# Expert weights in runs of 32 KB a partition, in pools opened on the mixer's bytes, in a hybrid encoder layer

## The chip, the cores and the metric

The kernel runs on one core of one Trainium2 chip. The metric is the device time of one execution in microseconds (us); the median of the runs counts. The engines are TensorE (PE in the rows; PEld is its weight load), VectorE (DVE), ScalarE (ACT), GpSimd (POOL) and SyncE (SP), whose queue issues nearly all transfers. Each transfer is spread over the core's 16 DMA engines.

## What is computed

One post-norm layer of an encoder on 512 tokens of 1024 columns, all in float32. A mixer (windowed attention and a short convolution, both gated) is followed by a LayerNorm and a routed mixture of 16 experts, in which each expert takes its 64 best tokens; a LayerNorm ends the layer.

```python
x = layer_norm(x, ln0_g, ln0_b)
h = hybrid_mixer(x, ...)                       # projections, attention, convolution, gates, output
x = layer_norm(DEEPNORM_ALPHA * x + h, ...)
aff = softmax(x @ w_router); top_val, top_idx = top_k(aff over tokens, 64)
xe = x[top_idx]                                # 16 experts x 64 tokens
h = silu(xe @ w_gate) * (xe @ w_up)            # 1024 -> 2048
ye = (h @ w_down) * top_val                    # 2048 -> 1024
x = layer_norm(DEEPNORM_ALPHA * x + scatter_add(ye, top_idx), ...)
```

The experts' weights are 16 x 3 x 8 MB, that is 402.7 MB, and each is read once.

## The kernel before, in words

**The mixer** streams its weights in chunks of 1 MB through two buffers called raw, splits each into a high and a low half (ws), and multiplies. Its tiles of 8 KB a partition have names: Z0 to Z3, Y0 to Y3, O0 to O3, M0 to M3, two raw, two ws; beside them stand X0 and X1 (the tokens), W0 to W2 (scratch), and E.

**The experts** are worked through in 8 pairs, one expert in each half of TensorE's columns. A pair has 48 weight units of 1 MB (8 KB a partition, 128 partitions). Units 0 to 31 are gate and up weights, in turn, in four blocks cb of eight; units 32 to 47 are the down weights, in four blocks cq of four. I number them on through the pairs, so that pair 1 begins with unit 48. For each unit `fetch` or `fetch_down` (lines 596 to 602) takes the next place of a list, `ring` (line 580), has SP load the unit into it (line 593), and TensorE multiplies it (line 933 for gate and up, 973 for down). The places of the ring are the mixer's tiles themselves, 20 of them, with E, W0 and W2; W0 and W2 are used once. Unit 0 goes into E, 1 to 4 into Z0 to Z3, 5 and 6 into ws, 7 and 9 into raw, 8 into W2, 10 into W0, 11 to 22 into Y, M and O and M3; unit 23 goes into E again, unit 24 into Z0, and so on round the ring. Two places leave it behind the first down block (line 984) and become `acc`, the sum of the experts' outputs. A load waits on SP until the last reader of its place is done, and since every load is pinned in program order on SP's one queue, the loads behind it wait too.

Between the units a list `pend` gives TensorE small pieces of other work: the gather of the next pair's tokens (line 869, two pieces ahead of the down units, the rest at the next pair's start), the transposes of the hidden rows (956), and the scatter of each finished down block (990) whose result VectorE adds to `acc` (995).

**The end.** In the last pair the last unit is loaded in three pieces, and the sums of the last 256 columns don't pass through `acc`: in cq 2 four multiplications with the identity (line 980) put `acc`'s last 256 columns into four PSUM tiles `ends`, one for each 128 tokens, and line 1007 adds the last scatter to them. The last LayerNorm reads them (1010 on), and SP and ACT store the rows.

Of the kernel before, what the change touches and what calls it, by code (L numbers as in the profile page):

```python
# [18 lines left out]
P = 128  # L19
D = 1024  # L20
# [17 lines left out]

@with_exitstack
def encoder_layer(ctx: ExitStack, tc: tile.TileContext, x, ln0r, ln0c, w_in, conv_w, sink, w_ao, w_co, w_out,  # L40
                  ln1r, ln1c, w_router, w_gate, w_up, w_down, ln2r, out):
    nc = tc.nc
    const = ctx.enter_context(tc.tile_pool(name="const", bufs=1))
    xpool = ctx.enter_context(tc.tile_pool(name="xpool", bufs=1))
# [23 lines left out]
    def pst(name):  # L68
        return psp.tile([P, 512], F32, tag="ps", name=name)
# [32 lines left out]
    iota = const.tile([P, CAP], F32, name="iota")  # L102
    nc.gpsimd.iota(iota, pattern=[[1, CAP]], base=1, channel_multiplier=0, allow_small_or_imprecise_dtypes=True)

    spools = {}
    for n in ("Z0", "M", "O", "Y", "raw", "ws", "Z"):
        spools[n] = ctx.enter_context(tc.tile_pool(name=f"p{n}", bufs=2 if n in ("raw", "ws") else 1))
    rawp, wsp = spools["raw"], spools["ws"]

    def slot(tag, shape, name, dt=F32):  # L110
        return shaped((xpool if tag[0] == "X" else spools.get(tag) or spools[tag[0]]).tile([P, 2048], dt, tag=tag, name=name), shape)

    class Pair:

# [462 lines left out]
    for t in range(NT):  # L577
        hooks[(f"gc{t // 2 + 1}_{t % 2}", 0)] = [entry(t)]

    ring = ["E"] + [f"Z{i}" for i in range(4)] + ["ws", "ws", "raw", "W2", "raw", "W0"] + "Y0 Y1 Y2 Y3 M0 M1 M2 O0 O1 O2 O3 M3".split()  # L580

    def ring_slot(shape, name):
        tag = ring.pop(0)
        pool = {"ws": wsp, "raw": rawp, "E": extra}.get(tag) or (wk if tag[0] == "W" else spools.get(tag) or spools[tag[0]])
        return tag, shaped(pool.tile([P, 2048], F32, tag=tag, name=name), shape)

    ahead = {}

    def load(src, key):
        tag, c = ring_slot(list(src.shape[1:]), "w_" + "_".join(map(str, key)))  # L590
        if tag[0] != "W":
            ring.append(tag)
        pin(nc.sync.dma_start(c, src))
        return c

    def fetch(p, cb, kq, i):
        key = (p, cb, kq, i)
        return ahead.pop(key) if key in ahead else load((w_gate, w_up)[i][p, cb, kq], key)

    def fetch_down(p, cq, fq):  # L600
        for f, n in ((0, 2), (2, 1), (3, 1)) if (p, cq, fq) == (NPAIR - 1, 3, 3) else ((0, 4),):
            yield load(w_down[p, cq, fq][:, :, f:f + n, :], (p, cq, fq, f, "d")), 4 * fq + f

    def early():
        ahead[0, 0, 0, 0] = fetch(0, 0, 0, 0)

    hooks[("gc3_0", 2)] = [early]

# [242 lines left out]
    nc.vector.tensor_tensor(tied, mask[:, NT - 1:, 1, :], counts[:, :, 1, :], OP.mult)  # L851
    nc.vector.tensor_tensor(place, place, tied, OP.add)

    def gather(p):
        e = slice(2 * p, 2 * p + 2)
        px = wkt(1 + 2 * p, [2048], f"px_{p}")
        xe = px[:, 0:1024].rearrange("p (k c) -> p k c", k=KT)
        ohT = px[:, 1024:1536]
        oh1 = px[:, 1536:2048].rearrange("p (t a c) -> p t a c", t=NT, a=2)
        for t in range(NT):  # L860
            nc.vector.tensor_tensor(oh1[:, t], iota[:, None, :].to_broadcast([P, 2, CAP]),  # L861
                                    place[:, t, e, None].to_broadcast([P, 2, CAP]), OP.is_equal)

        def take(k, n):
            def go():
                ps = pst(f"g_{p}_{k}")
                for i in range(n):
                    for t in range(NT):
                        pin(nc.tensor.matmul(ps[:, i * P:(i + 1) * P], xt[t][:, (k + i) * P:(k + i + 1) * P],  # L869
                                             oh1[:, t].rearrange("p a c -> p (a c)"), start=(t == 0), stop=(t == NT - 1)))  # L870
                dst = xe[:, k:k + n, :].rearrange("p k c -> p (k c)")
                if p:
                    nc.scalar.copy(dst, ps[:, :n * P])
                elif k % 2:
                    nc.vector.tensor_scalar(dst, ps[:, :P], cols[:, 2, k:k + 1], cols[:, 3, k:k + 1], op0=OP.mult, op1=OP.add)
                else:
                    nc.scalar.activation(dst, ps[:, :P], AF.Identity, bias=cols[:, 3, k:k + 1], scale=cols[:, 2, k:k + 1])
            return go

        def rest():  # L880
            nc.vector.tensor_tensor(oh1, oh1, aff[:, :, e, None].to_broadcast([P, NT, 2, CAP]), OP.mult)
            ps = pst(f"oht_{p}")
            for t in range(NT):
                pin(nc.tensor.transpose(ps[:, t * P:(t + 1) * P], oh1[:, t].rearrange("p a c -> p (a c)"), ident))
            nc.scalar.copy(ohT, ps)
        return xe, ohT, [take(k, 2 if p else 1) for k in range(0, KT, 2 if p else 1)] + [rest]
# [32 lines left out]
        nxt[2].pop(0)()  # L919
    for p in range(NPAIR):  # L920
        last = p == NPAIR - 1
        xe, ohT, takes = nxt
        pend[:0] = takes
        for cb in range(NCB):
            pss = [mmt(f"p{nm}_{p}_{cb}") for nm in "gu"]
            for kq in range(4):
                for i in range(2):
                    wt = fetch(p, cb, kq, i)
                    for k in range(2):
                        kk = 2 * kq + k  # L930
                        for a in range(2):
                            hs = slice(64 * a, 64 * a + 64)
                            pin(nc.tensor.matmul(pss[i][hs, :], xe[:, kk, hs], wt[:, a, k, :], start=(kk == 0), stop=(kk == KT - 1)))  # L933
                    for _ in range(2 * i if p == cb == 0 else 1 - i):
                        if pend:
                            pend.pop(0)()
            if p == 0 and cb == 1:
                ln1 = wkt(0, [2, D], "ln1")
                nc.scalar.dma_start(ln1[0:1], ln1r[None])
                pend.extend(spread(ln1))  # L940
                pend.append(affine)
            if last and cb == 1:
                ln2 = wkt(2, [2, D], "ln2")
                nc.scalar.dma_start(ln2[0:1], ln2r[None])
                pend.extend(spread(ln2))
            hb = tmpt([512], f"h_{p}_{cb}")
            nc.scalar.activation(hb, pss[0], AF.Silu)  # L947
            nc.vector.tensor_tensor(hb, hb, pss[1], OP.mult)  # L948

            def turn(cb=cb, hb=hb, p=p):  # L950
                if cb == 0:
                    hTs[p] = wkt(2 + 2 * p, [FF // P, P], f"hT_{p}")
                hT = hTs[p]
                ps = pst(f"ht_{p}_{cb}")
                for i in range(4):
                    pin(nc.tensor.transpose(ps[:, i * P:(i + 1) * P], hb[:, i * P:(i + 1) * P], ident))
                nc.scalar.copy(hT[:, 4 * cb:4 * cb + 4, :].rearrange("p k c -> p (k c)"), ps)

            pend.append(turn)
        if not last:  # L960
            nxt = gather(p + 1)
            for _ in range(2):
                nxt[2].pop(0)()
            flush()
        for cq in range(4):
            pd = mmt(f"d_{p}_{cq}")
            for fq in range(4):
                for wt, f0 in fetch_down(p, cq, fq):
                    for ft in range(wt.shape[2]):
                        f = f0 + ft  # L970
                        for a in range(2):
                            hs = slice(64 * a, 64 * a + 64)
                            pin(nc.tensor.matmul(pd[hs, :256], hTs[p][:, f, hs], wt[:, a, ft, :], start=(f == 0), stop=(f == 15)))  # L973
                for _ in range(2):
                    if pend:
                        pend.pop(0)()
                if last and cq == 2 and fq >= 2:
                    for t in range(2 * fq - 4, 2 * fq - 2):
                        ends.append(pst(f"end{t}")[:, :256])
                        pin(nc.tensor.matmul(ends[t], ident, acc[t // 2][:, t % 2, 768:1024], start=True, stop=False))  # L980
            ye = tmpt([256], f"ye_{p}_{cq}")
            nc.scalar.copy(ye, pd[:, :256])  # L982
            if p == 0 and cq == 0:
                acc = [ring_slot([2, D], f"acc{i}")[1] for i in range(2)]

            def scatter(t, p=p, cq=cq, ye=ye, ohT=ohT):
                def go():
                    cs = slice(cq * 256, (cq + 1) * 256)
                    ps = (mmt if p == NPAIR - 1 and cq == 2 else pst)(f"sc_{p}_{cq}_{t}")
                    pin(nc.tensor.matmul(ps[:, :256], ohT[:, t * P:(t + 1) * P], ye, start=True, stop=True))  # L990
                    a = acc[t // 2][:, t % 2, cs]
                    if p == 0:
# [11 lines left out]


    for t in range(NT):
        pin(nc.tensor.matmul(ends[t], ohT[:, t * P:(t + 1) * P], ye, start=False, stop=True))
    for t in range(NT + 1):
        if t < NT:
            pin(nc.vector.bn_stats(st2[:, t, 3, :], ends[t]))  # L1010
# [84 lines left out]
```

## Time and profile before

| | |
|---|---|
| median of 3 runs | 1471.23 us (1469.98 to 1474.84) |
| the profiled execution | 1471.5 us, of it a span of 1469.8 us from the first to the last instruction |
| TensorE busy | 1386.3 us, 94% of the span |
| DMA | 451.13 MB, mean 307 GB/s |
| chain that ended last | PE 49%, DMA 47% |
| loads of the experts' weights | 383 of 1 MB or less in the rows by kind, median 19.9 us from issue to landing |

A busy TensorE in this profile is not TensorE at its peak: the ends of multiplications are modelled. What bounds a stage is read from the rate of the DMA engines in it and from what the engines' waits ended with.

### The profile page before, as it was taken

What the parts mean: (1) busy time and instruction counts of PE and PEld (TensorE: products, weight loads), DVE (VectorE), ACT (ScalarE), POOL (GpSimd) and SP (SyncE); (2) the same over time, 40 slices, a digit from 0 to 9 for tenths busy, and PEclk for the clock granted to TensorE, in tenths of its full rate; (3) what the DMA queues carried; (4) which work ended last, traced back from release to release, by engine and by line L of the source; (5) the groups of instructions that cost most, each with busy time, mean ns of one, the idle gap of its engine ahead of it and who ended that gap; (6) DMA issues with size and microseconds to landing.
All of it is one profiled execution on the core that took longest, in us unless ns stands there. A gap on an engine that the chain in (4) does not pass through costs nothing.

```text
span 1469.8 us, 18064 instructions
## 1 busy us (share of the span) xinstructions
PE 1386.3 (94%) x7559; PEld 810.6 (55%) x7559; DVE 396.8 (27%) x892; ACT 291.8 (20%) x580; POOL 61.8 (4%) x46
## 2 busy tenths in 40 slices
PE   8999999999999999999999998998998899899985
PEld 6878778788888843643644632542452353264243
DVE  7566656633335530110110110110010011010015
ACT  5654454422233211000001000000000000000100
POOL 3000000320000004000000000000000000000001
PEclk9999999999999999999999999999999999999998
DMA  4221222322237879999999999999999999999993
GB/s 146 97 76 58 87 86 87 115 99 102 86 143 295 327 297 379 419 419 420 419 419 420 418 419 420 419 419 420 419 420 419 419 419 420 419 419 419 420 420 153
DMA packets 67205, 451.13 MB, mean 307 GB/s; under 512 B 7730, under 2 KB 10418, under 8 KB 13234
## 3 DMA queue, kind: packets, MB, share of 16 engines
q1 hardware_dynamic: 65824, 446.28, 75.1%
q10 hardware_dynamic: 1300, 3.70, 0.7%
q8 instruction: 59, 0.97, 0.3%
q14 instruction: 22, 0.18, 0.0%
HBM read 447.86 MB, written 2.10 MB: 306 GB/s over the span
## 4 chain that ended last, share of the span: by engine, by line
PE 49%; DMA 47%; DVE 3%; ACT 1%; issue 0%; SPq 0%; DVEq 0%
DMA w<-in_w_gate 26%; DMA w_d<-in_w_down 14%; DMA w<-in_w_up 7%; PE d L973 5%; PE pu L933 4%; PE pg L933 4%; PE p_x L181 3%; PE p_b L181 3%; PE p_c L181 3%; PE p_q L181 3%; PE p_co L181 3%; PE p_ao L181 3%; PE p_gc L181 3%; PE p_ga L181 3%; PE g L869 2%; PE o L521 1%
## 5 line engine op out<-in xcount | busy, mean ns | idle before, releaser
L933 PE MATMUL pg<-w,px 128*64 128x512 f32 x1024 | 245.0, 598 | 33.1 <-DMA w<-in_w_gate 32.8
L933 PE MATMUL pu<-w,px 128*64 128x512 f32 x1024 | 246.9, 603 | 15.3 <-DMA w<-in_w_up 15.3
L973 PE MATMUL d<-w_d,hT 128*64 128x256 f32 x2048 | 237.7, 383 | 7.4 <-DMA w_d<-in_w_down 7.3
L973 PEld LDWEIGHTS d<-w_d,hT 128*64 128x64 f32 x2048 | 142.7, 137 | 94.4 <-issue 19.0
L933 PEld LDWEIGHTS pg<-w,px 128*64 128x64 f32 x1024 | 69.1, 136 | 192.4 <-issue 101.3
L933 PEld LDWEIGHTS pu<-w,px 128*64 128x64 f32 x1024 | 64.7, 136 | 145.6 <-issue 96.7
L995 DVE TENSOR_TENSOR acc<-acc,sc 128x256 f32<-128x256 f32 x108 | 45.5, 421 | 330.5 <-PE sc L990 330.1
L948 DVE TENSOR_TENSOR h<-h,pu 128x512 f32<-128x512 f32 x32 | 22.0, 688 | 344.7 <-PE pu L933 344.7
L947 ACT ACTIVATE h<-pg 128x512 f32<-128x512 f32 x32 | 19.1, 597 | 331.5 <-PE pg L933 331.5
L990 PE MATMUL sc<-ye,px 128*128 128x256 f32 x248 | 73.8, 411 | 0.0
L869 PEld LDWEIGHTS g<-px,xn 128*128 128x128 f32 x512 | 59.0, 192 | 20.5 <-issue 17.9
L982 ACT COPY ye<-d 128x256 f32<-128x256 f32 x32 | 11.9, 372 | 276.7 <-PE d L973 276.7
L990 PEld LDWEIGHTS sc<-ye,px 128*128 128x128 f32 x248 | 40.8, 188 | 43.7 <-issue 41.2
L869 PE MATMUL g<-px,xn 128*128 128x128 f32 x512 | 63.8, 280 | 0.2 <-DVE px L861 0.2
L181 PE MATMUL p_x<-yh,ws_x 128*128 128x512 f32 x128 | 43.9, 398 | 0.0
L181 PE MATMUL p_b<-yh,ws_b 128*128 128x512 f32 x128 | 43.9, 398 | 0.0
L181 PE MATMUL p_c<-yh,ws_c 128*128 128x512 f32 x128 | 43.7, 397 | 0.0
L181 PE MATMUL p_q<-yh,ws_q 128*128 128x512 f32 x128 | 42.1, 395 | 0.0
L493 ACT ACTIVATE pr<-pr,neg 128x256 f32<-128x256 f32 (+1 forms) x64 | 35.2, 553 | 28.7 <-DVE neg L489 28.7
L181 PE MATMUL p_ga<-yh,ws_ga 128*128 128x512 f32 x128 | 40.6, 391 | 0.0
L181 PE MATMUL p_gc<-yh,ws_gc 128*128 128x512 f32 x128 | 40.1, 389 | 0.0
L181 PE MATMUL p_ao<-oh,ws_ao 128*128 128x512 f32 x128 | 40.1, 389 | 0.0
(264 smaller groups left out, 1619.8 us busy)
## 6 DMA issues: line engine op xcount, KB each, us to landing
w<-in_w_gate SPq DMA_DIRECT2D x128, 1024.0 KB, 19.9
w<-in_w_up SPq DMA_DIRECT2D x128, 1024.0 KB, 19.9
w_d<-in_w_down SPq DMA_DIRECT2D x127, 1024.0 KB, 19.9
raw_q<-in_w_in SPq DMA_DIRECT2D x4, 1024.0 KB, 4.8
raw_c<-in_w_in SPq DMA_DIRECT2D x4, 1024.0 KB, 4.8
raw_x<-in_w_in SPq DMA_DIRECT2D x4, 1024.0 KB, 4.9
raw_b<-in_w_in SPq DMA_DIRECT2D x4, 1024.0 KB, 4.9
raw_ga<-in_w_in SPq DMA_DIRECT2D x4, 1024.0 KB, 4.7
```

The lines of the kernel that those rows point to most:

```text
L181: put(nc.tensor.matmul(ps, ws[:, a, k, :], (opnd.lo if b else opnd.hi)(k), start=(k + a + b == 0), stop=ends))
L493: nc.scalar.activation(p, p, AF.Exp, bias=self.neg[:, i:i + 1], accum_out=self.su[:, i:i + 1])
L521: nc.tensor.matmul(pa[half * 64:half * 64 + 64, :256], vt[g][:, self.b0 + j, :], self.pT[:, j, :, half, :], start=(j == 0), stop=(j == sel ...
L869: pin(nc.tensor.matmul(ps[:, i * P:(i + 1) * P], xt[t][:, (k + i) * P:(k + i + 1) * P], oh1[:, t].rearrange("p a c -> p (a c)"), start=(t ...
L933: pin(nc.tensor.matmul(pss[i][hs, :], xe[:, kk, hs], wt[:, a, k, :], start=(kk == 0), stop=(kk == KT - 1)))
L947: nc.scalar.activation(hb, pss[0], AF.Silu)
L948: nc.vector.tensor_tensor(hb, hb, pss[1], OP.mult)
L973: pin(nc.tensor.matmul(pd[hs, :256], hTs[p][:, f, hs], wt[:, a, ft, :], start=(f == 0), stop=(f == 15)))
L982: nc.scalar.copy(ye, pd[:, :256])
L990: pin(nc.tensor.matmul(ps[:, :256], ohT[:, t * P:(t + 1) * P], ye, start=True, stop=True))
L995: nc.vector.tensor_tensor(a, a, ps[:, :256], OP.add)
```

## The change

The three weight arrays become one, `w_moe`, laid out by pair and by group of four units, so that a group is one contiguous run of 32 KB in each partition (8 KB before).

- **Places.** The mixer's tiles get a pool each (ws and raw one each of two buffers), in the order Z0 to Z3, ws, raw, Y, M0 to M2, O, M3. Behind the routing all of them are closed, and on their bytes 20 places of 8 KB are opened: R0 and R1 in a pool that stays open, R2 to R19 in 18 pools of one. Every new tile waits for the tiles whose bytes it takes, not for whole pools ("reuse_waits").
- **Pair 0** goes on in units of 8 KB: 1 to 7 in R0 to R6, 8 in W2, 9 in R7, 10 in W0, 11 to 22 in R8 to R19, 23 in E, 24 to 41 in R2 to R19, 42 in E, 43 to 47 in R2 to R6. R0 and R1 take no second unit; they become `acc`.
- **From pair 1 on** R2 to R19 are closed and one pool of four buffers of 32 KB is opened there. A group of four units is one tile; its load of 4 MB is issued when its first unit is wanted. In the last pair, groups 4 to 11 are loaded by unit (8 KB a partition) into such a tile, and the last unit in three pieces as before.
- **The last sums.** The four multiplications with the identity become two of 512 columns, put into `pend` behind block cb 2 of the last pair; two blocks of 128 tokens share a PSUM tile. The scatters of the last pair's cq 2 take their PSUM from the other pool.

```diff
-    for n in ("Z0", "M", "O", "Y", "raw", "ws", "Z"):
-        spools[n] = ctx.enter_context(tc.tile_pool(name=f"p{n}", bufs=2 if n in ("raw", "ws") else 1))
+    mixer = ExitStack()
+    for n in "Z0 Z1 Z2 Z3 ws raw Y0 Y1 Y2 Y3 M0 M1 M2 O0 O1 O2 O3 M3".split():
+        spools[n] = mixer.enter_context(tc.tile_pool(name=f"p{n}", bufs=2 if n in ("raw", "ws") else 1))
...
+    UNITS = 48
+    units, groups = {}, {}
+
+    def load_unit(p, m, pool, tag):
+        t = pool.tile([P, 2048], F32, tag=tag, name=f"w_{p}_{m}")
+        pin(nc.sync.dma_start(t, w_moe[p, m // 4][:, m % 4]))
+        return t
+
+    def fetch(p, m):
+
+        if p == 0:
+            if m not in units:
+                units[m] = load_unit(0, m, *places.pop(0))
+            return units.pop(m)
+        g, j = m // 4, m % 4
+        if j == 0:
+            t = big[0].tile([P, 4, 2048], F32, tag="G", name=f"w_{p}_{g}")
+            src = w_moe[p, g]
+            if p < NPAIR - 1 or g < 4:
+                pin(nc.sync.dma_start(t, src))
+            for i in range(4 if p == NPAIR - 1 and g >= 4 else 0):
+                if (g, i) != (UNITS // 4 - 1, 3):
+                    pin(nc.sync.dma_start(t[:, i], src[:, i]))
+                else:
+                    ends, begin = shaped(t[:, i], [2, 4, 256]), shaped(src[:, i], [2, 4, 256])
+                    for f, n in ((0, 2), (2, 1), (3, 1)):
+                        pin(nc.sync.dma_start(ends[:, :, f:f + n, :], begin[:, :, f:f + n, :]))
+            groups[p, g] = t
+        return groups[p, g][:, j]
...
+    mixer.close()
+    small = ExitStack()
+    accp = ctx.enter_context(tc.tile_pool(name="accp", bufs=1, reuse_waits="tile"))
+    slots = [accp, accp] + [small.enter_context(tc.tile_pool(name=f"r{i}", bufs=1, reuse_waits="tile")) for i in range(18)]
+    slots = [(pool, f"R{i}") for i, pool in enumerate(slots)]
+    places = slots[:7] + [(wk, "W2")] + slots[7:8] + [(wk, "W0")] + slots[8:] + [(extra, "E")] + slots[2:] + [(extra, "E")] + slots[2:]
+    big = []
...
+        if p == 1:
+            small.close()
+            big.append(ctx.enter_context(tc.tile_pool(name="big", bufs=4, reuse_waits="tile")))
...
-                    wt = fetch(p, cb, kq, i)
+                    wt = shaped(fetch(p, 8 * cb + 2 * kq + i), [2, 2, 512])
...
+            if last and cb == 2:
+                def begin(i):
+                    def go():
+                        ps = pst(f"end{i}")
+                        pin(nc.tensor.matmul(ps, ident, acc[i][:, :, 768:1024], start=True, stop=False))
+                        ends.extend(ps[:, 256 * t:256 * t + 256] for t in range(2))
+                    return go
+                pend.extend(begin(i) for i in range(2))
...
-                if last and cq == 2 and fq >= 2:
-                    for t in range(2 * fq - 4, 2 * fq - 2):
-                        ends.append(pst(f"end{t}")[:, :256])
-                        pin(nc.tensor.matmul(ends[t], ident, acc[t // 2][:, t % 2, 768:1024], start=True, stop=False))
...
-                acc = [ring_slot([2, D], f"acc{i}")[1] for i in range(2)]
+                acc = [shaped(accp.tile([P, 2048], F32, tag=f"R{i}", name=f"acc{i}"), [2, D]) for i in range(2)]
...
-                    ps = (mmt if p == NPAIR - 1 and cq == 2 else pst)(f"sc_{p}_{cq}_{t}")
+                    ps = pst(f"sc_{p}_{cq}_{t}")
...
-        pin(nc.tensor.matmul(ends[t], ohT[:, t * P:(t + 1) * P], ye, start=False, stop=True))
+        pin(nc.tensor.matmul(ends[t], ohT[:, t * P:(t + 1) * P], ye, start=False, stop=(t % 2 == 1)))
```

## Rows read from the trace of the kernel before

**Rows 1.** The page: engines' busy time, GB/s in 40 slices, chain by engine.
```profile
PE 1386.3 (94%) x7559; PEld 810.6 (55%) x7559; DVE 396.8 (27%) x892; ACT 291.8 (20%) x580; POOL 61.8 (4%) x46
...
GB/s 146 97 76 58 87 86 87 115 99 102 86 143 295 327 297 379 419 419 420 419 419 420 418 419 420 419 419 420 419 420 419 419 419 420 419 419 419 420 420 153
...
PE 49%; DMA 47%; DVE 3%; ACT 1%; issue 0%; SPq 0%; DVEq 0%
```

**Rows 2.** Stretches: length, engines' busy time, granted clock, DMA share, GB/s.
```profile
523.10:529.20 6.10, 5.94 (x33) 3.03 (x34) 1.88 (x8) 0.46 (x1) 0.00 (x0) 1.00 0.02 4
600.00:1400.00 800.00, 748.58 (x4340) 339.05 (x4338) 75.97 (x170) 58.30 (x120) 0.00 (x0) 1.00 1.01 419
1443.00:1446.50 3.50, 3.50 (x25) 2.25 (x24) 1.51 (x4) 0.00 (x0) 0.00 (x0) 1.00 0.33 114
1446.50:1450.00 3.50, 3.50 (x31) 2.18 (x31) 1.50 (x4) 0.00 (x0) 0.00 (x0) 1.00 0.00 0
...
1455.00:1460.00 5.00, 0.00 (x0) 0.00 (x0) 4.90 (x12) 1.48 (x2) 2.46 (x2) 0.70 0.28 107
```

**Rows 3.** TensorE's waits for weights: us in total, times, longest.
```profile
PE pg L933 <- DMA w<-in_w_gate: 32.8, 62, 1.4
...
PE pu L933 <- DMA w<-in_w_up: 15.3, 27, 0.9
...
PE d L973 <- DMA w_d<-in_w_down: 7.3, 15, 0.7
```

**Rows 4.** SP's queue in pair 0: start, us, line, tile, count.
```profile
528.24 0.33 SPq L593 DMA_DIRECT2D w<-in_w_up  x1
...
555.00 35.05 SPq L593 DMA_DIRECT2D w_d<-in_w_down  x16
592.18 0.33 SPq L593 DMA_DIRECT2D w<-in_w_gate  x1
```

**Rows 5.** TensorE in order of time, pair 0 and the starts of pairs 1, 2.
```profile
526.26 1.94 PE L933 MATMUL pg<-w,px 128*64 128x512 f32 x8
...
599.71 8.85 PE L973 MATMUL d<-w_d,hT 128*64 128x256 f32 x80
608.50 1.13 PE L990 MATMUL sc<-ye,px 128*128 128x256 f32 x4
...
612.49 5.40 PE L973 MATMUL d<-w_d,hT 128*64 128x256 f32 x48
...
631.15 3.67 PE L973 MATMUL d<-w_d,hT 128*64 128x256 f32 x32
634.66 1.89 PE L933 MATMUL pg<-w,px 128*64 128x512 f32 x8
...
739.18 1.89 PE L933 MATMUL pg<-w,px 128*64 128x512 f32 x8
```

**Rows 6.** All DMA packets from 528.2 to 600 us.
```profile
DMA packets 3630, 26.50 MB, mean 369 GB/s; under 512 B 398, under 2 KB 398, under 8 KB 398
```

**Rows 7.** SP's DMA queue, 600 to 1400 us: packets, MB, share of 16 engines.
```profile
q1 hardware_dynamic: 45968, 334.77, 100.9%
```

**Rows 8.** The same queue, 1446.5 to 1469 us: the stores, 2 KB packets.
```profile
q1 hardware_dynamic: 864, 1.57, 18.1%
```

**Rows 9.** ACT's DMA queue, 212.6 to 217.5 us: tokens in 4 KB packets.
```profile
q10 hardware_dynamic: 288, 1.05, 64.6%
```

**Rows 10.** TensorE at the end, in order of time.
```profile
1429.32 1.95 PE L973 MATMUL d<-w_d,hT 128*64 128x256 f32 x16 [0.43 <-DMA w_d<-in_w_down]
...
1437.08 1.13 PE L980 MATMUL end<-acc,ident 128*128 128x256 f32 x4
...
1446.95 3.67 PE L973 MATMUL d<-w_d,hT 128*64 128x256 f32 x32
1451.10 1.99 PE L1007 MATMUL end<-ye,px 128*128 128x256 f32 x8 [0.47 <-ACT ye L982]
```

More of the change, by code (lines that the diff above doesn't have):

```diff
@@ L40, in encoder_layer @@
 def encoder_layer(ctx: ExitStack, tc: tile.TileContext, x, ln0r, ln0c, w_in, conv_w, sink, w_ao, w_co, w_out,
-                  ln1r, ln1c, w_router, w_gate, w_up, w_down, ln2r, out):
+                  ln1r, ln1c, w_router, w_moe, ln2r, out):
     nc = tc.nc
@@ L105, in encoder_layer @@
     spools = {}
-    for n in ("Z0", "M", "O", "Y", "raw", "ws", "Z"):
-        spools[n] = ctx.enter_context(tc.tile_pool(name=f"p{n}", bufs=2 if n in ("raw", "ws") else 1))
+    mixer = ExitStack()
+    for n in "Z0 Z1 Z2 Z3 ws raw Y0 Y1 Y2 Y3 M0 M1 M2 O0 O1 O2 O3 M3".split():
+        spools[n] = mixer.enter_context(tc.tile_pool(name=f"p{n}", bufs=2 if n in ("raw", "ws") else 1))
     rawp, wsp = spools["raw"], spools["ws"]
     def slot(tag, shape, name, dt=F32):
-        return shaped((xpool if tag[0] == "X" else spools.get(tag) or spools[tag[0]]).tile([P, 2048], dt, tag=tag, name=name), shape)
+        return shaped((xpool if tag[0] == "X" else spools[tag]).tile([P, 2048], dt, tag=tag, name=name), shape)
     class Pair:
@@ L578, in encoder_layer @@
         hooks[(f"gc{t // 2 + 1}_{t % 2}", 0)] = [entry(t)]
[L580 to L602, printed above, removed]
+    UNITS = 48
[24 more added lines that the diff above has]
+        return groups[p, g][:, j]
     def early():
-        ahead[0, 0, 0, 0] = fetch(0, 0, 0, 0)
+        units[0] = load_unit(0, 0, extra, "E")
     hooks[("gc3_0", 2)] = [early]
@@ L967, in encoder_layer @@
             for fq in range(4):
[L968 to L973, printed above, removed]
+                wt = shaped(fetch(p, 32 + 4 * cq + fq), [2, 4, 256])
+                for ft in range(4):
+                    f = 4 * fq + ft
+                    for a in range(2):
+                        hs = slice(64 * a, 64 * a + 64)
+                        pin(nc.tensor.matmul(pd[hs, :256], hTs[p][:, f, hs], wt[:, a, ft, :], start=(f == 0), stop=(f == 15)))
                 for _ in range(2):
@@ L1064, in per_partition @@
         return np.stack([r.reshape(KT, P).T for r in rows], axis=1)
+    both = np.stack([a[n][0].reshape(NPAIR, 2, 4, 2, P, NCB, 512).transpose(0, 5, 2, 4, 1, 3, 6) for n in ("w_gate", "w_up")], axis=3)
+    both = both.reshape(NPAIR, NCB, 2, 2, 2, P, 2048).transpose(0, 1, 2, 5, 3, 4, 6).reshape(NPAIR, 2 * NCB, P, 4, 2048)
     lay = {
@@ L1078 @@
         "w_router": a["w_router"][0].reshape(KT, P, NE).transpose(1, 0, 2),
-        "w_gate": a["w_gate"][0].reshape(NPAIR, 2, 4, 2, P, NCB, 512).transpose(0, 5, 2, 4, 1, 3, 6),
-        "w_up": a["w_up"][0].reshape(NPAIR, 2, 4, 2, P, NCB, 512).transpose(0, 5, 2, 4, 1, 3, 6),
-        "w_down": a["w_down"][0].reshape(NPAIR, 2, 4, 4, P, 4, 256).transpose(0, 5, 2, 4, 1, 3, 6),
+        "w_moe": np.concatenate([both, a["w_down"][0].reshape(NPAIR, 2, 4, 4, P, 4, 256).transpose(0, 5, 4, 2, 1, 3, 6)
+                                 .reshape(NPAIR, 4, P, 4, 2048)], axis=1),
         "ln2r": np.stack([a["ln2_g"][0], a["ln2_b"][0]]),
```

## The prediction, made before the changed kernel was run

> **What bounds the kernel now.** Read the page first: TensorE is busy 94% of the span, yet the chain that ended last is 47% DMA, and from the 17th slice on the GB/s stand at 419 to 420 without a break [rows 1]. Then the stretches: from 600 to 1400 us the DMA engines are busy with a share of 1.01, and TensorE lacks 51 us of work [rows 2]. The waits say for what: for weights, 55 us in 104 waits, none over 1.4 us [rows 3]. So from about 600 us to the end, time is bytes over rate, and TensorE follows. TensorE's own need is shown by pair 1, when it was still behind the loads and had no wait: from 634.66 to 739.18, 104.5 us a pair [rows 5]. The queue of SP moved 334.77 MB in 800 us [rows 7], which is 2.506 us for a unit of 1 MB (1.0486e6 bytes), 120.3 us for a pair's 48. TensorE has 13% to spare.
>
> Pair 0 is another stage. When TensorE reaches its first unit at 526.26 [rows 5], 23 units lie loaded and the DMA engines do nothing (4 GB/s from 523 to 529 [rows 2]); from then on a load is issued when TensorE gives a place back, the first at 528.24 [rows 4]. Bytes began to move at about 529.2, 0.96 us behind the issue. What counts is the lead: at 592.18 SP already issues pair 1's first unit, 48, while TensorE begins pair 0's down units only at 599.71 [rows 4, 5]. From 528.2 to 600 the engines moved 26.50 MB [rows 6], 25.3 units on top of 23: pair 1's first unit began to move at 599.3. TensorE wanted it at 634.66. That lead of 35 us is what the places buy.
>
> **The change, step by step.** The sum is made against the profiled execution: 1471.5 us, span 1469.8; the median is 1471.23, so no correction is needed.
>
> *The change of pools, pair 0 to 1.* This is the largest term, and it is a loss. By the code, the pool of four runs begins where R2 began, and I take its first run to lie on its first buffer: R2 to R5. Their last tenants in pair 0 are units 43 to 46, the third round of the places. Unit 46 is the last but one that TensorE reads: the two units at 631.15 take until 634.66, so it is done at 632.9 [rows 5]. TensorE has no wait in pair 0 before, and will have none after (below), so that time stands. SP then issues the first run at 632.9, and bytes move at 633.9, where before they moved at 599.3: **+34.6 us**. Behind that waiting issue SP holds the other three runs; two of them lie on places read out long before (units 32 to 35 at 606.7, four of the five at 599.71; units 36 to 39 at 616.0 [rows 5]), and can't pass. Nothing else is on SP's queue until the stores. TensorE stands from 634.7 until the run has landed, some 9.8 us behind 633.9, at about 644. Its clock will fall meanwhile (0.70 in the mean of 1455 to 1460, when the last multiplication had ended at 1453.1 [rows 2, 10]); the restart at half the clock costs TensorE at most the 11 us of one run's work, which its 13% take back while DMA goes on: nothing on the path.
>
> *Two places fewer in pair 0.* R0 and R1 wait for `acc`, so unit 24 is issued when unit 3 is read, not unit 1. With the release times of the queue I get landings up to 3.5 us later through unit 47, which then lands at about 604 and is wanted at 632.9. Hidden by 29 us.
>
> *Runs of 32 KB.* They are used in pairs 1 to 6 and four groups of pair 7: 76 runs, 304 units; the other 32 units of pair 7 and pair 0 stay at 8 KB. No row shows a 32 KB packet from memory. A packet of 8 KB costs 100.9% of 16 x 800 us over 40,865 packets, 316 ns [rows 7]; a packet of 2 KB, in the stores, 18.1% of 16 x 22.5 us over 767, 85 ns [rows 8]. A line through both has 38.5 ns for each KB and 8 ns fixed. One 32 KB packet for four saves 24 of 1264 ns, 1.9%: 304 x 2.506 x 1.9% = **-14.5 us**. Ends: nothing, if the time goes by bytes alone; the 4 KB packets, 198 ns [rows 9], would make the fixed part 80 ns and the gain 146 us, but those loads came alone and paid their start in the share, and the slope left would be 29 ns a KB, far from any rate here. I take the 2 KB row's, with up to twice as much as open. Below nothing I bound it by the same 14.5.
>
> Of the price of a transfer the Trainium skill says, in "DMA: Bandwidth & Descriptors", section "Bandwidth", that a DMA costs about 2.0 us and its bytes, so that larger ones pay. By that, joining four would save 6 us a run; the row has 2.506 us for a whole unit, so in this queue that cost is overlapped and the rule's sum doesn't apply.
>
> *Coarser buffers.* The run behind the next three is issued when TensorE has read a run out, 8.7 us of work in the mean (104.5 over 12) where a run takes 9.8 to load. Some 20 us of loads are then still queued. Nothing, while TensorE keeps its clock.
>
> *The end.* The last weight bytes came between 1443 and 1446.5 [rows 2], but TensorE ended its down units at about 1450.6: from 1429.32 it had no wait, and in cq 2 it carried the four multiplications with the identity, twice 1.06 us [rows 10]. Moved into the gate block cb 3 they stand beside waits for weights. The last eight units then need 8 x 1.76 + 8 x 0.53 = 18.3 us, under the 20 of their loads, so TensorE ends some 0.8 us behind the last landing (a quarter of a unit, 0.44, and its start), not 4.1: **-3.3 us**. The shared PSUM tiles make the first statistics wait for a second multiplication, a quarter of the 1.99 us at 1451.10: +0.4.
>
> Sum: 34.6 - 14.5 - 3.3 + 0.4 = +17.2, so 1488.7; I say **1488 us**.
>
> **The rivals.**
> (a) *Runs bring nothing*, or the array's wider pitch (32 KB from partition to partition) takes back what packets give: 1503. For it: the DMA share is 1.01 already. The Trainium skill, "DMA: Bandwidth & Descriptors", section "Latency and other measured facts", has copies slowed by row pitches of large powers of two, from 512 KiB on; no run here shows pitch.
> (b) *Runs bring twice the line's gain* (16 ns fixed): 29 us, 1474, within the noise. The Trainium skill, the same page, puts the ports' ceiling at 435.2 GB/s; an estimate from that is 29 us too.
> (c) *The first run lies on places read out early*, the third or fourth buffer first: issued at 606.7 or 616.0. Then two runs keep DMA busy until the rest is free at 634.7; of the 34.6 about 17 remain: 1471. Against it: the code's order of bytes.
> (d) *It does what it says, faster.* If the first runs wait for no unit of the third round, at places R2 to R5 as released by units 24 to 27 (before 590), there is no stop: 3.5 - 14.5 - 2.9 = -14, 1458. It decides at an issue before 616: from there on the stop is less than the 17.4 us gained. Against it: units 43 to 46 must be read from those bytes, and they are.
> (e) *TensorE becomes the bound.* Waits come in one piece per run, up to 9.8 - 4 x 1.72 = 2.9 us in a gate run, and its clock falls in each. With 2 us lost a run, gate runs still fit, the 28 runs of down units (8.7 us) lack 0.9 each: 25 us, 1514. Against it: the clock held 1.00 through 600 to 1400 [rows 2].
>
> **How the numbers follow.** Chances: forecast 0.55, (a) 0.12, (b) 0.10, (c) 0.08, (d) 0.08, (e) 0.07. The range from 1470 to 1503 leaves out (d) and (e), 0.15. A measurement of this kernel tells 0.3%, 4.4 us, from no change. Slower: the forecast, (a) and (e), 0.74. Same: (b) and (c), 0.18. Faster: 0.08.
>
> **What will show it.** GB/s near 0 from about 604 to 634, and SP's first load of a run at 632.9; TensorE idle from 634.7 to 644 and the clock down there; then a rate above 419, 427 by the line, to the end; waits of TensorE of 1 to 3 us, one a run, clock 1.00; at the end down units less than 1.5 us behind the last landing. I am wrong if a run is issued well before 632.9, if the rate stays at 419 or passes 432, or if DMA stops again later.

## The result, and the profile after

| | before | after |
|---|---|---|
| median | 1470.84 us (1469.98 to 1474.84, 4 runs) | 1484.38 us (1483.78 to 1485.54, 4 runs) |
| the profiled execution | 1471.5 us | 1484.66 us, of it a span of 1483.0 |

The ratio is 1.0088 (95% interval 1.0068 to 1.0107): slower, by 13.5 us in the medians and 13.2 us in the spans. 1488 had been predicted. The page of the changed kernel (busy time of the engines; GB/s in 40 slices of the span, here of 37.1 us; the chain that ended last, by engine) answers to [rows 1]:

```profile
PE 1383.1 (93%) x7555; PEld 815.9 (55%) x7555; DVE 397.0 (27%) x892; ACT 291.8 (20%) x580; POOL 62.0 (4%) x46
...
GB/s 148 105 63 57 86 85 86 117 110 85 114 114 354 299 5 418 344 393 426 435 426 432 429 430 431 429 432 429 432 430 429 433 426 434 427 434 426 417 419 176
...
PE 56%; DMA 40%; DVE 3%; ACT 1%; issue 0%; SPq 0%; DVEq 0%
```

Three things differ. One whole slice, the 15th, has 5 GB/s; the 17th and 18th have 344 and 393. From the 19th to the 37th the rate stands at 426 to 435, where it was 419; the 38th and 39th, with the last pair's loads of 1 MB, have 417 and 419. The stretches tell where the two holes lie (length, busy time of PE, PEld, DVE, ACT and POOL, granted clock, DMA share, GB/s), as [rows 2] did for before:

```profile
523.10:555.00 31.90, 31.74 (x174) 15.04 (x174) 4.08 (x12) 3.60 (x7) 0.00 (x0) 1.00 0.01 1
555.00:622.00 67.00, 67.00 (x392) 30.88 (x390) 6.33 (x15) 7.38 (x14) 18.58 (x8) 1.00 1.00 413
622.00:633.60 11.60, 11.60 (x98) 7.25 (x95) 1.68 (x4) 0.37 (x1) 0.00 (x0) 1.00 0.15 60
634.00:644.00 10.00, 0.38 (x4) 0.00 (x0) 0.89 (x4) 0.37 (x1) 0.00 (x0) 0.78 0.86 370
644.00:660.00 16.00, 15.15 (x72) 7.34 (x72) 0.69 (x1) 0.74 (x2) 0.00 (x0) 0.82 1.03 446
660.00:1340.00 680.00, 622.08 (x3618) 287.41 (x3618) 63.17 (x141) 47.78 (x98) 0.00 (x0) 0.99 1.00 430
```

The hole that had been predicted is the second one, and it ends where it should: bytes move again at 633.6. But it begins at about 623.6 and not at 604 (60 GB/s over the 11.6 us behind 622 are 0.7 MB, 1.7 us of full rate), since there was a first hole, from 523 to 555, that no step of the prediction had. The kernel before has the first 6 of these 32 us too [rows 2]; 26 are new. SP's queue in order of time (start, us from the first to the last, line, tile, count), as [rows 4]:

```profile
454.65 151.24 SPq L589 DMA_DIRECT2D w<-in_w_moe  x47
632.70 120.75 SPq L603 DMA_DIRECT2D w<-in_w_moe  x15
```

Pair 0's 47 loads behind unit 0 are issued until 605.9, and the first run at 632.70, against a forecast of 632.9. What SP's queue waited for (us in total, times, longest):

```profile
SPq L603 <- PE pu L955: 404.5, 48, 13.9
SPq L603 <- PE d L1003: 232.1, 26, 9.7
...
SPq L589 <- DMA ln<-in_ln1r: 44.0, 1, 44.0
```

The last row is the first hole: one load of pair 0, unit 21, stood 44.0 us until another load had landed, the 8 KB row of the last LayerNorm's weights, which has nothing to do with it. (The row goes as one packet of 8 KB, on one DMA engine, and not over all 16 as the loads of weights do.) That row is issued from ScalarE's queue, into W0, and so not before unit 10, the tenant of W0, has been read:

```profile
552.84 0.49 ACTq L961 DMA_DIRECT2D ln<-in_ln1r  x1
```

TensorE at the change of pairs, in order of time (start, us, line, operation, count, and in brackets the idle time before with what ended it), as [rows 5]:

```profile
630.71 3.67 PE L1003 MATMUL d<-w,hT 128*64 128x256 f32 x32
644.85 3.68 PE L955 MATMUL pg<-w,px 128*64 128x512 f32 x8 [10.47 <-DMA w<-in_w_moe]
```

It stands 10.47 us for the first run; its first unit then takes 3.68 us, where one takes 1.94 otherwise: the granted clock had fallen (0.78 in the mean of 634 to 644, 0.82 of 644 to 660), and from 660 on it is 0.99.

The rate in the steady part, from SP's DMA queue between 660 and 1340 us (packets, MB, share of 16 engines), first of the kernel before:

```profile
q1 hardware_dynamic: 39082, 284.62, 100.9%
```

and of the changed kernel:

```profile
q1 hardware_dynamic: 10027, 292.03, 100.0%
```

In 680 us these are 418.55 and 429.46 GB/s, or 2.5053 and 2.4416 us for a unit: 0.0637 us less.

At the end, the GB/s of 40 slices between 1453 and 1464 us (0.275 us each), and below them TensorE in order of time, as [rows 10]:

```profile
GB/s 399 309 257 227 253 216 231 220 238 238 209 238 149 142 201 216 209 197 179 171 190 183 179 153 48 48 45 48 41 15 0 0 0 0 0 0 0 0 0 0
```

```profile
1453.90 1.95 PE L1003 MATMUL d<-w,hT 128*64 128x256 f32 x16 [0.55 <-DMA w<-in_w_moe]
1455.78 1.13 PE L1016 MATMUL sc<-ye,px 128*128 128x256 f32 x4
1456.84 1.95 PE L1003 MATMUL d<-w,hT 128*64 128x256 f32 x16
1458.71 1.13 PE L1016 MATMUL sc<-ye,px 128*128 128x256 f32 x4
1459.77 3.67 PE L1003 MATMUL d<-w,hT 128*64 128x256 f32 x32
1463.92 1.99 PE L1033 MATMUL end<-ye,px 128*128 128x256 f32 x8 [0.47 <-ACT ye L1008]
```

The last bytes land at 1461.2 (30 slices of 0.275), and TensorE ends its down units at 1463.4, 2.2 us later; before, it was 4.1. The four multiplications with the identity no longer stand there.

The balance of the two traces: pair 1's bytes begin 34.3 us later (633.6 against 599.3); 304 units in packets of 32 KB give back 304 x 0.0637 = 19.4; the lag behind the last landing gives 1.9; the tail from there to the end of the span takes 19.6 where it took 19.2. 34.3 - 19.4 - 1.9 + 0.4 = 13.4, against 13.2 in the spans.

### The profile page after: what moved, and what is told of

Its sections match the earlier page's. It is cut to its first block, busy times and chain, and to the rows that moved or that the text cites. A ratio compares the mean times of both kernels' runs of the same rounds, so it can differ in the third digit from the quotient of the medians.

```text
span 1483.0 us, 17525 instructions
## 1 busy us (share of the span) xinstructions
PE 1383.1 (93%) x7555; PEld 815.9 (55%) x7555; DVE 397.0 (27%) x892; ACT 291.8 (20%) x580; POOL 62.0 (4%) x46
## 4 chain that ended last, share of the span: by engine, by line
PE 56%; DMA 40%; DVE 3%; ACT 1%; issue 0%; SPq 0%; DVEq 0%
DMA w<-in_w_moe 39%; PE pu L955 7%; PE pg L955 7%; PE d L1003 6%; PE p_x L183 3%; PE p_b L183 3%; PE p_c L183 3%; PE p_q L183 3%; PE p_co L183 3%; PE p_ao L183 3%; PE p_gc L183 3%; PE p_ga L183 3%; PE sc L1016 2%; PE o L523 1%; PE s L483 1%; PE pt L510 1%
## 5 line engine op out<-in xcount | busy, mean ns | idle before, releaser
L955 PE MATMUL pg<-w,px 128*64 128x512 f32 x1024 | 250.7, 611 | 59.0 <-DMA w<-in_w_moe 58.7
L1003 PE MATMUL d<-w,hT 128*64 128x256 f32 x2048 | 238.4, 383 | 12.7 <-DMA w<-in_w_moe 12.1
L1003 PEld LDWEIGHTS d<-w,hT 128*64 128x64 f32 x2048 | 142.9, 137 | 100.4 <-issue 29.8
L955 PEld LDWEIGHTS pg<-w,px 128*64 128x64 f32 x1024 | 72.4, 139 | 212.6 <-issue 167.6
L1064 POOL TENSOR_TENSOR acc<-acc,ln 128x512 f32<-128x512 f32 x2 | 3.2, 1641 | 882.7 <-ACT acc L1061 882.7
```

## The experiments

The theory: the loss is one wait, that of the first run for the third round of the places; the 44 us wait lies in its shadow; the gain is the fixed cost of packets. The rivals: the 44 us wait is the loss; the first run's place doesn't matter; the rate has another source than the packet, the load of 4 MB or the layout.

| kernel | median us | ratio to before (95%) | span us |
|---|---|---|---|
| the change | 1484.38 | 1.0088 (1.0068 to 1.0107) | 1483.0 |
| ln1_gpsimd | 1486.73 | 1.0110 (1.0095 to 1.0126) | 1483.0 |
| third_round_r6 | 1474.08 | 1.0028 (1.0015 to 1.0041) | 1471.9 |
| r6_and_ln1 | 1467.27 | 0.9978 (0.9965 to 0.9991) | 1465.8 |
| runs_in_8kb | 1506.19 | 1.0245 (1.0230 to 1.0260) | 1504.2 |
| runs_in_16kb | 1491.07 | 1.0135 (1.0120 to 1.0151) | 1489.1 |
| early_places | 1459.38 | 0.9925 (0.9910 to 0.9939) | 1457.1 |
| early_tail | 1464.32 | 0.9956 (0.9941 to 0.9971) | 1463.0 |
| early_fine | 1460.14 | 0.9922 (0.9909 to 0.9935) | 1458.0 |
| sums_only | 1469.50 | 0.9990 (0.9980 to 1.0001) | 1467.6 |

### Is the 44 us wait the loss? (ln1_gpsimd)

```diff
-                nc.scalar.dma_start(ln1[0:1], ln1r[None])
+                nc.gpsimd.dma_start(ln1[0:1], ln1r[None])
```

> The changed kernel with one line altered: the row of the last LayerNorm's weights (8 KB) is loaded from GpSimd's queue and not from ScalarE's, so that no load on SP shares its completion with it. The whole layer is computed. In the changed kernel SP stood 44.0 us on that landing and the DMA engines stopped twice, from 523 to 555 and from 622 to 634. My theory: that first stop is slack, because the first run must wait for unit 46 at 632.7 in any case. The first stop goes, the units of pair 0 are all landed at about 604, the second stop grows to some 30 us (604 to 633.6), SP's first run stays at 632.7, and the time stays at 1484, within 2 us. Rival (the 44 us wait is what the change costs): the loads behind it come 20 to 30 us earlier, the first run with them, and the time falls to 1455 to 1465.

Measured: the same span, 1483.0 us; the median is 2.3 us higher, with intervals that overlap. The stretches of this kernel (columns as above):

```profile
523.00:555.00 32.00, 31.84 (x176) 15.09 (x176) 3.97 (x11) 3.60 (x7) 0.66 (x1) 1.00 0.63 231
...
600.00:604.00 4.00, 4.00 (x40) 2.66 (x38) 0.00 (x0) 0.00 (x0) 0.00 (x0) 1.00 0.35 143
604.00:622.00 18.00, 18.00 (x140) 11.11 (x138) 3.37 (x8) 0.74 (x2) 0.00 (x0) 1.00 0.00 1
622.00:633.60 11.60, 11.60 (x96) 7.28 (x94) 1.69 (x4) 0.37 (x1) 0.00 (x0) 1.00 0.12 30
```

and SP's first run, in the queue's rows:

```profile
632.44 120.75 SPq L603 DMA_DIRECT2D w<-in_w_moe  x15
```

The first hole is gone, and the second begins at about 601.3 instead of 623.6; SP's first run is issued at 632.44. The hole has moved, not shrunk: one event, the reading of unit 46, ends it in both kernels. The wait of 44 us, the longest of SP's in that stage, costs nothing here. That it is gone with the row's queue also fits its cause, which the built program has: the loads of SP and of ScalarE count their landings on eight semaphores, taken in turn in the program's order, whichever of the two queues issues them. In the changed kernel the row stands between units 13 and 14 in that order, unit 21 is the next load on the same semaphore, and it waits for the row's count. Issued by GpSimd, the row counts on a semaphore of another kind, and unit 21 follows unit 13.

### Is the first run's place the loss? (third_round_r6)

```diff
-    places = ... + slots[2:] + [(extra, "E")] + slots[2:]
+    places = ... + slots[2:] + [(extra, "E")] + slots[6:]
```

> The changed kernel with the places of one round altered: pair 0's units 43 to 47 go into R6 to R10 and not R2 to R6, so that the bytes of the first run (R2 to R5) hold units 24 to 27 last, which are read out before 590. The whole layer is computed. My theory (the stop is the first run's wait for the third round): SP issues the first run right behind unit 47, at about 606 instead of 632.7; DMA runs on through 622, where the changed kernel stopped until 633.6, and the second run (R14 to R17, units 36 to 39) follows; what stays of the stop is some us around 634, when the next place comes free. The 44 us wait stays and has become part of the path. Time 1473.6, that is 10.8 under the changed kernel. Rival (the first run's place isn't the cause, SP or the pool holds the run until TensorE ends pair 0 all the same): 1484, first run at 632 or later.

Measured: 1474.08, 10.3 us under the change. SP's queue and the stretches in this kernel:

```profile
607.60 144.44 SPq L603 DMA_DIRECT2D w<-in_w_moe  x16
```

```profile
523.00:555.00 32.00, 31.84 (x176) 15.07 (x176) 3.99 (x11) 3.60 (x7) 0.00 (x0) 1.00 0.01 1
...
604.00:622.00 18.00, 18.00 (x141) 11.11 (x138) 3.37 (x8) 0.74 (x2) 0.00 (x0) 1.00 1.01 420
622.00:633.60 11.60, 11.60 (x98) 7.26 (x94) 1.69 (x4) 0.37 (x1) 0.00 (x0) 1.00 1.04 443
633.60:645.00 11.40, 10.40 (x64) 5.64 (x62) 1.23 (x5) 1.07 (x3) 0.00 (x0) 1.00 1.00 431
```

One slice bound in a list, four places further, and the first run is issued 25 us earlier. The 10.3 us are about the length of the second hole (623.6 to 633.6). From 555 on the DMA engines don't stop again, not even near 634, where I had expected some us. The loss that is left is the first hole, which has lost its shadow.

### Both together (r6_and_ln1)

> Both edits together: pair 0's units 43 to 47 in R6 to R10, and the last LayerNorm's row loaded from GpSimd's queue. The whole layer is computed. My theory: with the first run free early and no wait of 44 us, the first run is issued at about 603, the second when units 36 to 39 are read at 616, the third and fourth when unit 47 (on R10) is read at 634.5; two short stops of DMA between them are left, some 15 us in all instead of 34. Time 1466.5, 18 under the changed kernel and 4 under the kernel before. If the two edits only add up with no dependence on each other, and the second is worth nothing alone (first rival), 1473.6. If the stop were not the cause of the loss (second rival), 1484.

Measured: 1467.27, 17.1 us under the change, and 0.2% under the kernel before. One edit alone gave nothing and the other 10.3, so 6.8 us come from the two together. Its stretches:

```profile
523.00:555.00 32.00, 31.84 (x174) 14.93 (x174) 4.38 (x13) 3.60 (x7) 0.66 (x1) 1.00 0.62 225
...
600.00:604.00 4.00, 4.00 (x40) 2.67 (x38) 0.00 (x0) 0.15 (x1) 0.00 (x0) 1.00 0.73 258
604.00:622.00 18.00, 18.00 (x140) 11.11 (x138) 3.28 (x8) 0.74 (x2) 0.00 (x0) 1.00 0.93 383
622.00:633.60 11.60, 11.60 (x97) 7.26 (x94) 1.78 (x5) 0.37 (x1) 0.00 (x0) 1.00 0.43 183
633.60:645.00 11.40, 11.40 (x72) 6.21 (x70) 1.59 (x5) 1.12 (x3) 0.00 (x0) 1.00 0.88 351
```

Against 430 GB/s, the four stretches from 600 to 645 lack 1.6, 2.0, 6.7 and 2.1 us. That is the rest of the loss. The third run lies from R10 on, and waits for unit 47, the fourth stands behind it, and both are issued only at 634.61. The longest of SP's waits for down units is the third run's:

```profile
SPq L603 <- PE d L1003: 254.1, 26, 18.2
```

### What is the gain? (runs_in_8kb, runs_in_16kb)

Each run as four loads of 1 MB, in packets of 8 KB:

```diff
-            if p < NPAIR - 1 or g < 4:
+            if False:
                 pin(nc.sync.dma_start(t, src))
-            for i in range(4 if p == NPAIR - 1 and g >= 4 else 0):
+            for i in range(4):
```

> The changed kernel with the same tiles, places and order, but each run of four units loaded by four loads of 1 MB in packets of 8 KB (32 KB and one load of 4 MB before). The whole layer is computed. My theory (the gain in rate, 429.5 against 418.6 GB/s, is the packets' size): the rate from 660 to 1340 falls back to 419 GB/s, 304 units cost 0.0636 us more each, +19.3, so about 1503.7. First rival (the rate comes from the new layout of the weights in memory or from fewer waits of SP, not the packet): the rate stays at 429 and the time at 1484. Second rival (finer loads let TensorE begin pair 1 earlier and matter more than the packets): under 1484.

or as two of 2 MB, in packets of 16 KB:

```diff
             if p < NPAIR - 1 or g < 4:
-                pin(nc.sync.dma_start(t, src))
+                for i in (0, 2):
+                    pin(nc.sync.dma_start(t[:, i:i + 2], src[:, i:i + 2]))
```

> The changed kernel with each run loaded by two loads of 2 MB, in packets of 16 KB. The whole layer is computed. My theory (a fixed cost for each packet): of the 0.0636 us a unit that packets of 32 KB save, two thirds stay (half of the packets against three quarters removed); the rate from 660 to 1340 is 425.8 GB/s and the time 1484.4 + 6.4 = 1491. Rival (the gain is in one load having 4 MB, not in the packet): two loads for each run keep little or none, 1500 or more. Second rival (the packets are full speed from 16 KB on): 1484.

Measured: 1506.19 and 1491.07, with SP's DMA queue between 660 and 1340 us of the first

```profile
q1 hardware_dynamic: 42352, 283.97, 101.1%
```

and of the second

```profile
q1 hardware_dynamic: 19885, 289.65, 100.4%
```

These are 417.6 and 426.0 GB/s; 425.8 had been expected of the second. In the same places and from the same arrays, the 8 KB packets are back at the rate of before, and nothing is left of the gain. (The first edit does a little more than was meant: the last unit of every pair, and not of the last pair alone, now comes in three pieces, in packets of 2 and 1 KB. By the times of these packets in the trace such a unit takes 0.44 us longer, 2.6 us for the six of pairs 1 to 6. That is the 2.5 by which the time lies above the 1503.7 expected, and the 0.2% by which the rate lies under that of before.) A unit takes 2.4617 us in 16 KB packets, 0.0436 less than the 2.5053 in 8 KB packets of before, which is 68% of the 0.0637 that 32 KB give; they remove half of the packets where 32 KB remove three quarters, which is 67% of that. A run in 8 KB packets has 24 more of them on each DMA engine and takes 4 x 0.0637 = 0.255 us more, 10.6 ns each.

But packets of 32, 16 and 8 KB also mean one, two and four loads for a run, in the same proportion: by the rates alone the price could be that of a load. The packets' own times in the traces tell them apart. In the means of the same 680 us a packet of SP's queue takes 315.0 ns with 8 KB before and 315.1 in runs_in_8kb, 616.5 with 16 KB and 1219.5 with 32 KB. These lie on one line, 301.5 ns for each 8 KB and 13.5 ns for each packet, and the layout of the arrays makes no difference to it. A load adds one packet of 4 B on each engine, 9.0 ns. So the 8 KB run costs an engine 24 x 13.5 = 324 ns for packets and 3 x 9.0 = 27 ns for loads; at most one part in thirteen of the price is the load's, the rest is the packet's. That the clock shows 255 ns and not 351 agrees with the shares: with 100.9% the packets of 8 KB overlap by some 0.09 us a run, with 100.0% those of 32 KB don't.

### Each run on bytes read out early (early_places)

With the row on GpSimd's queue, and the places dealt by when their last tenant is read:

```diff
-    places = ... + slots[2:] + [(extra, "E")] + slots[2:]
+    places = ... + slots[:10] + slots[14:18] + slots[10:14] + slots[18:] + [(extra, "E")] + slots[6:9]
```

> The changed kernel with the last LayerNorm's row on GpSimd's queue and the places of pair 0 dealt so that each run finds its bytes read out early: units 24 to 33 in R0 to R9, 34 to 37 in R14 to R17 (the second run), 38 to 41 in R10 to R13 (the third), 42 and 43 in R18 and R19, 44 in E, 45 to 47 in R6 to R8 (the fourth). The whole layer is computed. My theory: the first run is issued right behind unit 47, at about 603.5, the second and third when units 37 and 41 are read, and about 7 us of stops are left of 34.3; time 1457, that is 27 under the changed kernel, 10 under the kernel with both single edits (1467) and 14 under the kernel before. Rival (the third round of the places costs elsewhere, since R0 and R1 must be read before acc opens, or a later wait of SP takes the gain): 1467 or more.

Measured: 1459.38, 25.0 us under the change, and 0.75% under the kernel before. Its stretches:

```profile
523.00:555.00 32.00, 31.84 (x175) 15.18 (x176) 3.83 (x10) 3.60 (x7) 0.66 (x1) 1.00 0.80 294
555.00:600.00 45.00, 45.00 (x220) 17.20 (x218) 2.96 (x7) 6.63 (x12) 18.60 (x8) 1.00 0.88 348
600.00:604.00 4.00, 4.00 (x40) 2.70 (x38) 0.00 (x0) 0.00 (x0) 0.00 (x0) 1.00 0.67 223
604.00:622.00 18.00, 18.00 (x142) 11.09 (x140) 3.37 (x8) 0.74 (x2) 0.00 (x0) 1.00 1.04 447
622.00:633.60 11.60, 11.60 (x98) 7.25 (x96) 1.69 (x4) 0.37 (x1) 0.00 (x0) 1.00 0.98 417
633.60:645.00 11.40, 11.40 (x70) 6.04 (x68) 1.59 (x5) 1.12 (x3) 0.00 (x0) 1.00 0.92 368
```

The bytes run on through the change of pairs almost without a stop: against 430 GB/s, 600 to 604 lacks 1.9 us, 622 to 645 another 2.0. Of the 34.3 us, 25.9 are recovered in the span; 27 had been expected. This kernel is faster than both.

### Where else runs pay, and where not (early_tail, early_fine)

In the last pair, groups 4 to 9 as runs too:

```diff
-            if p < NPAIR - 1 or g < 4:
+            if p < NPAIR - 1 or g < 10:
...
-            for i in range(4 if p == NPAIR - 1 and g >= 4 else 0):
+            for i in range(4 if p == NPAIR - 1 and g >= 10 else 0):
```

> As the kernel with the places dealt for early runs, and in the last pair groups 4 to 9 are loaded as runs of 4 MB too, so that 8 units and not 32 stay at 1 MB. The whole layer is computed. My theory (a 32 KB packet saves 0.0636 us a unit, wherever it lies): 24 units more, -1.5 us, 1455.5 if the places give 1457. Rival (TensorE, which stands close behind the loads in the last pair, gets its units later in a coarse run and is still behind at the last eight): no gain or up to 3 us more.

Measured: 1464.32, 4.9 us above the kernel with the places alone. The rival decides, by more than the 3 us that it allowed. TensorE at the end of this kernel:

```profile
1415.27 1.95 PE L1003 MATMUL d<-w,hT 128*64 128x256 f32 x16 [1.89 <-DMA w<-in_w_moe]
...
1439.80 3.67 PE L1003 MATMUL d<-w,hT 128*64 128x256 f32 x32
```

At 1415.27 a run has just landed whole, with 12 units still to be multiplied: from there TensorE works without a wait to 1443.5, though the last bytes land at about 1435. A unit inside a run can be used only when all four are there, and near the end no time is left to make that good.

The other way, with the last pair all in units:

```diff
-            if p < NPAIR - 1 or g < 4:
+            if p < NPAIR - 1:
...
-            for i in range(4 if p == NPAIR - 1 and g >= 4 else 0):
+            for i in range(4 if p == NPAIR - 1 else 0):
```

> As the kernel with the places dealt for early runs, and the whole last pair is loaded by units of 1 MB (16 more than there). The whole layer is computed. With 24 units more in runs the time had risen by 5 us, since TensorE waited for a whole run and had no time left to catch up. My theory: 16 units in packets of 8 KB cost 16 x 0.0636 = 1.0 us more of loading, and TensorE, which was without a wait from 1360 to its end and finished some 4 us behind the last landing, ends about 2.2 us behind it as in the changed kernel; 1458.5, and in the profile waits of TensorE for weights of about 0.5 us a unit among the last twelve units. Rival (how far TensorE lies behind at the end isn't set by the runs of the last pair's first groups): only the 1.0 us remains, 1460.4, and TensorE's last twelve units stay without waits.

Measured: 1460.14, 0.8 us above the kernel with the places alone, and 0.9 in the span. By the times the two can't be told apart (the intervals of their ratios to before nearly coincide); the spans, of one execution each, agree with the 1.0 us of smaller packets. I had misread the other kernel's end: by its GB/s in slices the last bytes land at 1435.3 and TensorE ends at 1437.7, 2.4 us later and not 4. So there was nothing to win back, as the rival had it. The waits that the theory wanted are there all the same, and buy nothing:

```profile
1428.75 1.95 PE L1003 MATMUL d<-w,hT 128*64 128x256 f32 x16 [0.53 <-DMA w<-in_w_moe]
```

Four groups of runs in the last pair, as the change has them, and none are alike within the noise; ten cost 4.9 us.

### The last sums alone (sums_only)

The kernel before with the two multiplications of 512 columns behind block cb 2:

```diff
+            if last and cb == 2:
+                ...
+                pend.extend(begin(i) for i in range(2))
...
-                if last and cq == 2 and fq >= 2:
-                    ...
-                        pin(nc.tensor.matmul(ends[t], ident, acc[t // 2][:, t % 2, 768:1024], start=True, stop=False))
```

> The kernel before with one part of the change alone: the last sums begun as two multiplications of 512 columns behind gate block cb 2 of the last pair, two blocks of tokens to a PSUM tile, and the scatters of cq 2 from the other pool. The whole layer is computed. My theory: TensorE ends its down units 2.1 us sooner, the first statistics start 0.4 later; 1.5 to 2 us under the kernel before, about 1469. Rival (TensorE at the end is held by the last loads, not by these multiplications, or the shared tiles' statistics cost as much as they bring): no difference, 1471.

Measured: 1469.50, 1.7 us under the kernel before, with an interval that reaches 1.0001, so in the times it is hardly told from nothing; the span is 2.2 us shorter. TensorE's last scatter begins at

```profile
1448.54 1.99 PE L1011 MATMUL end<-ye,px 128*128 128x256 f32 x8 [0.47 <-ACT ye L986]
```

where it was 1451.10 before [rows 10]. This part of the change is worth about 2 us by the profile.

## Why the prediction was right, point by point

**The change of pools** (+34.6) was right, in its cause, its place and its size: SP's first run at 632.70 (632.9 forecast), bytes 34.3 us later, TensorE idle for 10.47 us with its clock down. It was read from the order of bytes in the code and from one column of the trace, the time at which TensorE finishes the last tenant of each place. third_round_r6 shows the cause: with another tenant there the issue moves from 632.70 to 607.60.

**Two places fewer** was right in its result and wrong in its way. Unit 47 was to land at 604, hidden by 29 us; it landed at about 623.6, and some 9 us were left. The places themselves were counted well enough: without the row's wait (ln1_gpsimd) pair 0's bytes end at about 601.3. But the step counted only the places and not the semaphores of the loads. In the trace of before no load waits for this row: there it stands between units 28 and 29 in the turn, and the next load on its semaphore, unit 36, comes behind its landing. A wait of the same kind was in that trace all the same, for the other LayerNorm row that ScalarE issues:

```profile
SPq L593 <- DMA ln<-in_ln2r: 1.4, 1, 1.4
```

That the 44 us were free was luck: the larger stop covered them. With that stop removed (third_round_r6 against r6_and_ln1) it costs 6.8 us, and a prediction of that kernel by the same steps would have missed it.

**Runs of 32 KB** (-14.5) was too small: 19.4. The mechanism, a fixed cost for each packet, held, and runs_in_16kb gave it to within 0.2 GB/s. The term that was mis-sized is that cost, 8 ns from a line through packets of 2 KB and 8 KB, against 10.6 measured. The line had 38.5 ns for each KB, where the loads have 37.7 (301.5 for 8): its 2 KB row was of stores, the nearest there was, and the price was wanted for loads. Rival (b), twice the gain, had 16 ns, and rival (a), nothing, is excluded by runs_in_8kb. The Trainium skill has its 2.0 us for each DMA in "DMA: Bandwidth & Descriptors", section "Anatomy of one DMA — SWDGE (gpsimd) path", for transfers of GpSimd's queue, and not in the section "Bandwidth" that the prediction names. By it each run joined would have saved 6 us; by the rates here it is 0.255 us.

**Coarser buffers** at nothing was right: the waits of the gate units, of their weight loads and of the down units in the changed kernel (us in total, times, longest) answer to [rows 3]:

```profile
PE pg L955 <- DMA w<-in_w_moe: 58.7, 36, 10.5
...
PEld pg L955 <- DMA w<-in_w_moe: 38.7, 19, 2.7
...
PE d L1003 <- DMA w<-in_w_moe: 12.1, 15, 1.6
```

Without the first run's 10.5 the 35 others in the first row take 1.4 us each, none in the second is over 2.7, and the granted clock from 660 to 1340 is 0.99, where 1.00 had been forecast. Rival (e) didn't come about (its price was also too high: pairs 1 to 6 have 24 runs of down units, not 28, since pair 7 loads them by unit). early_tail shows where the step ends: in the last pair, where no later slack can take the delay back.

**The end** (-3.3) was 1.9. The step took the scatters as an even 0.53 us for each unit. They come in the last four units twice 1.13: these need 9.5 us from 1453.90, and the last bytes land 7.3 us behind it. So the lag is 2.2 us, not 0.8, and over the 1.5 that had been named as a sign. The **shared PSUM tiles** cost the +0.4 that was forecast, by the length of the tail, 19.6 us against 19.2, one execution each.

Two errors, of 4.9 and 1.4 us, point against each other: the sum was 4 us too high. The condition of rival (d), runs on bytes that are read out before 590, isn't met by the change; early_places comes nearest to it, and has 1459.4 where (d) had 1458.

## What to carry to other kernels

When buffers are opened on the bytes of others, ask for each new buffer which tenant of its bytes is read last, and deal the old places so that the first new buffer falls on the one that is free first: here one bound in that list was worth 10.3 us, and a better order together with one small load on another queue 25.0, where the whole change had lost 13.5. A long wait can be free while a longer one ends later; before it is called harmless or the culprit, ask which event ends the stop. Join loads where a queue is never empty, since each packet has its price, but keep them small where the consumer has no slack left to wait for a whole one.

## What the runs showed that I had not expected

A small load on ScalarE's queue held SP's queue for 44.0 us, without sharing data or a place with it, and a change of the issuing queue took that away (ln1_gpsimd).

The price of a packet is 10.6 ns by the clock over a whole range: 8, 16 and 32 KB give 418.6, 426.0 and 429.5 GB/s. A line through them leaves little more to win by larger ones: without any packet cost a unit would take 2.4416 - 0.0212 = 2.420 us, 433 GB/s (an estimate from the three rates). The Trainium skill, in "DMA: Bandwidth & Descriptors", section "Where 436 GB/s comes from", puts the ceiling of the 16 ports at 435.2 GB/s; over 680 us the traces stay under it and come within 1.3%. (Short stretches come out higher, as the 447 over 18 us in early_places, but at a DMA share of 1.04: 16 packets of 32 KB more or less at their bounds make 29 GB/s there.)

In the last 8 us of weights the rate is half or less: 142 to 257 GB/s in the slices from 1453.5 to 1459.6, and under 50 from there to 1461.2 (the fence of the end above); in the kernel before, the last 3.5 us of weights went at 114 GB/s and a DMA share of 0.33 [rows 2]. Why the engines are not full there wasn't tried.
